# Preparing the down projection's weight sums one gate/up pair earlier in a fused block kernel

## The chip, the cores and the metric

The kernel runs on one core of a Trainium2 chip. The metric is the device time of one execution in microseconds (us), as a median of several runs; beside it stands one profiled execution, whose trace is what is read here.

## The reference

One layer of a streaming encoder on a sequence of 1024 rows with D = 1024, all in float32:

```
h  = rms_norm(x, norm1_w) * (1 + scale1) + shift1
x  = x + gate1 * hybrid_mixer(h, ...)          # gated delta rule + short conv, then w_out
h  = rms_norm(x, norm2_w) * (1 + scale2) + shift2
x  = x + gate2 * swiglu(h, w_gate, w_up, w_down)
return rms_norm(x, norm_f_w)

def swiglu(h, w_gate, w_up, w_down):
    return (jax.nn.silu(h @ w_gate) * (h @ w_up)) @ w_down
```

`shift`, `scale` and `gate` come from the vector c. w_gate and w_up are 1024 x 2816, w_down is 2816 x 1024. Everything that follows is in `swiglu`.

## The kernel before

**Products.** Every float32 operand is split into a high part (a cast to a rounded float32 that TensorE multiplies fast) and a low remainder; a product is three matmuls (high-high, high-low, low-high). A cast of the high part is ScalarE's (ACT), the subtraction that gives the low part VectorE's (DVE). The large matrix products are done by a seven-product scheme on 2 x 2 blocks (Strassen's in Winograd's form): sums of blocks (`S1` to `S4` of the left operand, `T1` to `T4` of the right) take the place of the eighth product.

**Gate and up.** The 2816 hidden columns are cut into `NP = 11` pairs of 128-column tiles. The loop `for p in range(1, NP)` goes through pairs 1 to 10, each in seven steps `s = 0..6`. A step loads (`turn_load`, `Weights.load`), sends the DMAs that were put on the list `pend` (`flush`), issues its matmuls (`run`, `inner`, `inner2`) and then `block(p, s)`, which is the work of the other engines after that step: closing the accumulators, SiLU, the gate-times-up product, and the casts and remainders for pair p + 1. The products of pair p go to the DRAM scratch `am_scr`, as left operands of the down projection.

**Down.** After pair 10 the down phase runs through three chunks of pairs (4, 4 and 3). Its right operands are blocks of w_down: a row pair j has the quarters B11, B12, B21, B22 (`quarter(j, i)`, i = 0..3, each 128 x 512), and

```
T1 = B12 - B11     T2 = T1 - B22     T3 = B12 - B22     T4 = B21 + T2
```

These lie in the DRAM scratch `bm[j, name]`. For row pairs 0 to 7 (`j < NRAW`) the weights stay as they are, since gate2 is applied to the output of the first two chunks; for row pairs 8 to 10 the weights are multiplied by gate2 (`row(i)`) first. Row pairs 0 to 8 are prepared in pieces within the gate/up loop, in pair p = j + 2; row pairs 9 and 10 within the down phase (`prep_load`, `prep_gate`, `prep_sums`).

**A piece** is `load_one_part(j, i)`, which loads quarter i into a buffer, and `part_of(i)`, which for i = 0 and 3 makes the negative (`neg`) and puts stores on `pend`. Additions are done by accumulating DMAs from GpSimd's queue (POOL): an entry of `pend` with three members is sent there, all others go through SyncE's queue (SP). `part_sums(j, n)` puts the sums on the list that need no tile (for raw row pairs B12 and B21 go from w_down to `bm` straight).

**Buffers.** The pieces use a ring of three tiles (`ring3`, `raw0` to `raw2`), in turn with other users: `turn_load(p - 3)` loads a tile of x, and `turn1(p - 3)` at the end of step 2 transposes it (a DVE instruction) into the next ring tile, from where four small DMAs write it out. A new user of a ring tile waits until the earlier one's reads and DMAs are done. In a regular pair the ring goes: part 0, x tile, transposed tile, part 3.

**Order.** Each engine works in the order in which the program issues to it; SP issues the DMAs in order too and waits at each one for what it needs. The weights of pair p + 1 are loaded by SP at steps 3 and 5 of pair p (`R<-in_w_gate`, `R<-in_w_up`).

Of the kernel before, what the change touches and what calls it, by code (L numbers as in the profile page):

```python
# [13 lines left out]
ALU = mybir.AluOpType  # L14
# [37 lines left out]
def kernel(  # L52
# [1567 lines left out]
    for n, m in enumerate((4, 5, 6, 7, 0, 1, 2, 3)):  # L1620
# [5 lines left out]
        if n in (0, 4, 7):  # L1626
            i = {0: 1, 4: 2, 7: 3}[n]
# [327 lines left out]
    def row(i):  # L1955
        return gates[5][:, i % 2 * HT:(i % 2 + 1) * HT]
# [4 lines left out]

    def part_of(i):
        j, t = bd[i]
        if j < NRAW:
            neg = t
        else:
            DVE.tensor_tensor(t, t, row(i), ALU.mult)
            neg = ring3() if i in (0, 3) else None
        if i in (0, 3):
            ACT.mul(neg, t, -1.0)  # L1970
        if i == 0:
            pend.append((bm[j, "T1"], neg))
        elif i == 1:
            pend.append((bm[j, "T3"], t))
            pend.append((bm[j, "T1"], t, 1))
        elif i == 3:
            pend.append((bm[j, "T2"], neg))
            pend.append((bm[j, "T3"], neg, 1) if j >= NRAW else (bm[j, "T3"], neg))
        else:
            pend.append((bm[j, "T4"], t))  # L1980
        if j >= NRAW and i != 1:
            pend.append((bm[j, {0: "B11", 2: "B21", 3: "B22"}[i]], t))

    def part_sums(j, n):
        b12, b21 = quarter(j, 1), quarter(j, 2)
        if n == 0 and j < NRAW:
            pend.extend([(bm[j, "T4"], b21), (bm[j, "T1"], b12, 1)])
        elif n == 1:
            if j < NRAW:
                pend.append((bm[j, "T3"], b12, 1))  # L1990
            pend.append((bm[j, "T2"], bm[j, "T1"], 1))
        elif n == 2:
            pend.append((bm[j, "T4"], bm[j, "T2"], 1))

    def prep_load(j, get):
        for fi in (0, 1):
# [20 lines left out]
    def block(p, s):  # L2017
        w, n = W.get(p), W.get(p + 1)
        last = p == NP - 1
        if s == 0:  # L2020
            if p > 0:
                o = p - 1
                a12 = c[o]["z5"][1]
                ACT.activation(a12, bk[o][0]["X"], AF.Silu)
                if w and p > 1:
                    w.cast("S2", 0)
                    w.cast("S2", 1)
                DVE.tensor_tensor(a12, bk[o][1]["X"], a12, ALU.mult)
                store(o, "A12", a12)
            if p == 1:  # L2030
                w.sum_n("S1")
                w.sum_n("S2")
                w.mat("S2")
            elif w:
                w.inner_low(2)
                w.inner_low(3)
                w.low("S2", 0)
                w.low("S2", 1)
                act(p - 1, "u2")
        elif s == 1:  # L2040
            if p < 2:
                keep(p, "p1", "X")
                rest0()
                w.cast("S1", 0)
                w.cast("S1", 1)
            elif w:
                w.sum_n("S4")
                w.sum_n("S1")
                w.mat("S1")
                sums_u2(p - 1)  # L2050
            if p > 0:
                o = p - 1
                a11, s1, a21 = c[o]["p1"][0], c[o]["p1"][1], c[o]["u2"][0]
                DVE.tensor_tensor(a11, a11, s1, ALU.subtract)
                DVE.tensor_tensor(a21, c[o]["z5"][1], a11, ALU.add)
                store(o, "S2", a11)
                store(o, "S4", a21)
            if p == 1:
                w.low("S1", 0)
                w.low("S1", 1)  # L2060
                w.sum_n("S3")
            if 1 < p < NP:
                part_of(0)
                part_sums(p - 2, 0)
            if p == 2:
                inner_t(1)
        elif s == 2:
            if p < 2:
                close(p, "p1", "Y")
            else:  # L2070
                close_inner(p, "p1")
            w.cast("S3", 0)
            silu(p, "p1")
            w.cast("S3", 1)
            w.low("S3", 0)
            w.low("S3", 1)
            act(p, "p1")
            store(p, "A11", c[p]["p1"][0])
            if p == 1:
                w.sum_n("S4")  # L2080
            if 3 <= p:
                turn1(p - 3)
        elif s == 3:
            keep(p, "u2", "X")
            if p >= FIRST2:
                w.inner_sums("S4")
                for i in range(4):
                    w.inner_cast(i)
                    w.inner_low(i)
                w.iu2 = w.iu  # L2090
            else:
                w.mat("S4")
            if p == 2:
                inner_t(2)
            if p == 3:
                inner_t(4)
        elif s == 4:
            keep(p, "z5", "Z")
            w.mat("A22")
            if p > 1:  # L2100
                if last:
                    part_of(1)
                else:
                    part_of(3)
                    part_sums(p - 2, 1)
            if n:
                n.mat("A11")
                if p != FIRST2:
                    n.sum_n("S3")
            if last:  # L2110
                first_mats(0, "A11", am_scr)
        elif s == 5:
            if p:
                close(p, "z5", "X")
            silu(p, "z5")
            act(p, "z5")
            if p == FIRST2:
                n.sum_n("S3")
            store(p, "A22", c[p]["z5"][0])
            if last:  # L2120
                part_of(3)
                part_sums(p - 2, 1)
                part_of(2)
            if p > 1:
                part_sums(p - 2, 2)
            if p == 2:
                inner_t(3)
            if last:
                first_mats(1, "B11", None)
        elif s == 6:  # L2130
            if p >= FIRST2:
                close_inner2(p)
            else:
                close(p, "u2", "Z")
            if n and p:
                n.inner_sums()
                n.inner_cast(0)
            elif n:
                n.cast("A12", 0)
            if p < FIRST2:  # L2140
                silu(p, "u2")
            if n and p:
                n.inner_cast(1)
                n.inner_low(0)
                n.inner_low(1)
            elif n:
                n.cast("A12", 1)
                n_slot[0] += 2
                n.low("A12", 0)
                n.low("A12", 1)  # L2150
            if n and p:
                n.inner_cast(2)
                n.inner_cast(3)
                n.sum_n("S2")
            if last:
                act(p, "u2")
                sums_u2(p)
            if last:
                first_mats(2, "A12", am_scr)
# [195 lines left out]

    for p in range(1, NP):
        for s in range(7):
            if p > 1 and s in (0, 3):
                load_one_part(p - 2, 1 if p == NP - 1 and s else s)
            if p == NP - 1 and s == 4:  # L2360
                load_one_part(p - 2, 3)
                load_one_part(p - 2, 2)
            if 3 <= p and s == 1:
                turn_load(p - 3)
            if s == 3 and p < NP - 1:
                W[p + 1] = Weights(p + 1)
                W[p + 1].load(0)
            if s == 5 and p < NP - 1:
                W[p + 1].load(1)
            if p == NP - 1 and s in (3, 5, 6):  # L2370
                first_load(*{3: (0, "A11"), 5: (1, "B11"), 6: (2, "A12")}[s])
            if s != 6 or p > 1:
                flush()
            if s == 1 and p > 1:
                keep(p, "p1", "X")
                inner(p, ("m1", "m2", "m5", "m6", "m3"))
            elif s == 2 and p > 1:
                run(p, s, (0,))
                inner(p, ("m7",))
                run(p, s, (1,))  # L2380
                inner(p, ("m4",))
            elif s == 5 and p >= FIRST2:
                inner2(p, ("m1", "m5", "m2", "m6", "m3", "m4"))
            elif s == 6 and p >= FIRST2:
                run(p, s, (0,), (0, 1))
                inner2(p, ("m7",))
                run(p, s, (0,), (2, 3))
                run(p, s, (1,))
            else:
                run(p, s)  # L2390
            block(p, s)
            if p == 1 and s in LATE:
                LATE[s]()
# [219 lines left out]
```

## Time and profile before

| | |
|---|---|
| median of 3 runs | 1151.91 us (1151.44 to 1152.65) |
| profiled execution | 1151.3 us, span 1149.5 us |
| busy: PE, its weight loads, DVE, ACT, POOL | 1136.6, 961.0, 962.4, 606.2, 92.3 us |
| pairs 1 to 10 of gate/up | about 556 to 930.5 us of the span |
| down phase | about 930.5 us to the end |

PE is TensorE, PEld its weight loads, SPq SyncE's queue. A row of the timeline gives a start, a duration, the engine, the operation, `out<-in` by the program's names (buffer numbers left out), and in brackets the idle time before it with what ended that. Steps of a pair last 5.4 us of PE, some with smaller matmuls a little more or less; pair 9 begins at 855.8 us and pair 10 at 893.2 us.

### The profile page before, as it was taken

To read this page: it belongs to the slowest core of one execution; us is meant where nothing else is said; L and a number is where in the kernel's file an instruction comes from. 1 tells how busy PE (TensorE), PEld (TensorE's weight loads), DVE (VectorE), ACT (ScalarE), POOL (GpSimd) and SP (SyncE) were. 2 spreads that over 40 slices of the span, in tenths; PEclk is the share of its full clock that TensorE was granted. 3 is DMA by queue.
4 is the path that set the end of the run, shared out by engine and by line. 5 is a ranking of instruction groups with operands and counts; after the bars stand their busy time and mean duration, and the time that the engine had idled before them with its cause. 6 is when DMAs were issued, how large, how long until landed. Compare 5 with 4: busy or idle time off the path is not lost.

```text
span 1149.5 us, 17231 instructions
## 1 busy us (share of the span) xinstructions
PE 1136.6 (99%) x5744; PEld 961.0 (84%) x5744; DVE 962.4 (84%) x1933; ACT 606.2 (53%) x1330; POOL 92.3 (8%) x129
## 2 busy tenths in 40 slices
PE   9999999999999999999999999999999999999997
PEld 7888888888888888888888888888888888888885
DVE  7898779799899787599989998878887977689976
ACT  7688743457743544255444545545455557454343
POOL 0001000100100101000000010101010000000302
PEclk9999999999999999999999999999999999999999
DMA  9931364743446582450336676866677599869933
GB/s 368 351 108 58 100 212 130 210 137 101 144 134 202 169 290 65 71 156 4 136 110 204 165 192 173 230 190 184 174 204 218 155 295 382 268 174 353 295 130 147
DMA packets 162634, 212.36 MB, mean 185 GB/s; under 512 B 54512, under 2 KB 79088, under 8 KB 162544
## 3 DMA queue, kind: packets, MB, share of 16 engines
q1 hardware_dynamic: 152656, 197.03, 52.7%
q0 software_dynamic: 7488, 13.63, 7.5%
q8 instruction: 45, 0.74, 0.3%
q10 hardware_dynamic: 2400, 0.59, 0.2%
q14 instruction: 45, 0.37, 0.1%
HBM read 161.40 MB, written 60.82 MB: 193 GB/s over the span
## 4 chain that ended last, share of the span: by engine, by line
PE 91%; DMA 4%; DVE 3%; ACT 1%; issue 1%; SPq 0%; POOL 0%; ACTq 0%; DVEq 0%; POOLq 0%
PE acc L87 34%; PE acc L449 24%; PE dn L87 18%; PE o L87 4%; PE o L449 3%; PE A L449 1%; PE K L449 1%; DMA raw<-in_w_in_dram 1%; DMA xbd<-dx 1%; PE w L449 1%; PE u L449 1%; PE qk L449 1%; PE kk L449 1%; DMA raw<-in_w_out_dram 1%; PE O L449 1%
## 5 line engine op out<-in xcount | busy, mean ns | idle before, releaser
L449 PE MATMUL acc<-h,u 128*128 128x512 f32 x1200 | 292.3, 396 | 0.0
L449 PEld LDWEIGHTS acc<-h,u 128*128 128x128 f32 x1200 | 220.9, 188 | 43.3 <-issue 0.5
L87 PE MATMUL acc<-h,hl 128*128 128x512 f32 (+1 forms) x540 | 109.0, 353 | 0.0
L87 PEld LDWEIGHTS acc<-h,hl 128*128 128x128 f32 x540 | 90.2, 189 | 15.0 <-issue 0.5
L87 PE MATMUL acc<-h,u 128*128 128x512 f32 (+1 forms) x516 | 100.3, 345 | 0.0
L87 PE MATMUL acc<-T,hl 128*128 128x512 f32 x408 | 97.5, 390 | 0.3 <-DVE T L88 0.3
L87 PEld LDWEIGHTS acc<-h,u 128*128 128x128 f32 x516 | 84.6, 189 | 12.6
L87 PE MATMUL dn<-h,h 128*128 128x512 f32 x396 | 91.5, 390 | 0.8 <-ACT h L88 0.6
L87 PE MATMUL acc<-T,u 128*128 128x512 f32 x384 | 91.1, 390 | 0.0
L87 PEld LDWEIGHTS dn<-h,h 128*128 128x128 f32 x396 | 74.2, 188 | 17.3 <-ACT h L88 1.0
L87 PEld LDWEIGHTS acc<-T,hl 128*128 128x128 f32 x408 | 75.3, 188 | 15.7 <-DVE T L88 0.8
L87 PEld LDWEIGHTS acc<-T,u 128*128 128x128 f32 x384 | 71.1, 188 | 13.9
L449 ACT CAST u<-raw 128x512 fp32r<-128x512 f32 x66 | 40.6, 620 | 57.1 <-PE acc L449 56.8
L449 DVE TENSOR_TENSOR u<-raw,u 128x512 fp32r<-128x512 f32 x82 | 55.9, 684 | 10.4 <-ACT u L449 10.2
L88 DVE TENSOR_TENSOR xo<-xo,dn 128x512 f32<-128x512 f32 x68 | 46.2, 682 | 14.8 <-PE dn L87 14.3
L88 ACT COPY L<-acc 128x256 f32<-128x256 f32 x68 | 25.3, 373 | 63.1 <-PE acc L87 62.8
L88 ACT CAST h<-rw 128x512 fp32r<-128x512 f32 x60 | 35.1, 620 | 40.8 <-PE dn L87 27.6
L449 DVE SCALAR_TENSOR_TENSOR cv<-pr,cols_a,cv 128x512 f32<-128x512 f32 x72 | 52.8, 746 | 1.7 <-ACT cv L449 1.5
L449 DVE SCALAR_TENSOR_TENSOR raw<-raw,cb 128x512 f32<-128x512 f32 x64 | 43.7, 682 | 10.9 <-DMA raw<-in_w_mod_dram 10.9
L88 DVE TENSOR_TENSOR h<-rw,h 128x512 fp32r<-128x512 f32 x60 | 39.5, 686 | 12.4 <-ACT h L88 12.4
L88 DVE TENSOR_TENSOR cc<-cc,acc 128x512 f32<-128x512 f32 x66 | 41.3, 644 | 6.7 <-PE acc L87 6.7
L88 ACT COPY cc<-acc 128x512 f32<-128x512 f32 x64 | 35.1, 583 | 19.8 <-PE acc L87 19.8
(391 smaller groups left out, 2222.3 us busy)
## 6 DMA issues: line engine op xcount, KB each, us to landing
raw<-in_w_in_dram SPq DMA_DIRECT2D x82, 256.0 KB, 3.0
am_scr<-cc SPq DMA_DIRECT2D x75, 256.0 KB, 2.1
raw<-in_w_mod_dram SPq DMA_DIRECT2D x64, 256.0 KB, 3.2
rw<-am_scr SPq DMA_DIRECT2D x53, 256.0 KB, 5.3
R<-in_w_gate_dram SPq DMA_DIRECT2D x22, 512.0 KB, 5.3
R<-in_w_up_dram SPq DMA_DIRECT2D x22, 512.0 KB, 5.7
rw<-bm SPq DMA_DIRECT2D x43, 256.0 KB, 5.3
wa<-in_w_mod_dram SPq DMA_DIRECT2D x16, 512.0 KB, 9.8
```

Of the source, the lines that this page charges most:

```text
L87: return call(*a, **k)
L88: ins = call(*a, **k)
L449: ins = call(*a, **k)
```

## The change

Row pairs 0 to 7 are prepared in pair p = j + 1 instead of j + 2, so row pair 0 in pair 1, where nothing was prepared before. Row pair 8, the gated one, was prepared as a whole in pair 10; now parts 0 and 1 come in pair 9, and parts 3 and 2 in pair 10. For it the negative is no longer ACT's, made from the gated tile, but DVE's, made from the raw tile in one instruction (times -1, times gate) into its own ring tile, ahead of the multiplication in place. For raw row pairs ACT's negation in place stays.

```diff
     def part_of(i):
         j, t = bd[i]
+        neg = t
         if j < NRAW:
-            neg = t
+            ACT.mul(t, t, -1.0)
         else:
+            if i in (0, 3):
+                neg = ring3()
+                DVE.scalar_tensor_tensor(neg, t, -1.0, row(i), ALU.mult, ALU.mult)
             DVE.tensor_tensor(t, t, row(i), ALU.mult)
-            neg = ring3() if i in (0, 3) else None
-        if i in (0, 3):
-            ACT.mul(neg, t, -1.0)
...
+    def part_step(p, n):
+        j = min(p - 1, NRAW)
+        if p == 1:
+            if n == 1:
+                part_of(0)
+                part_sums(j, 0)
+            elif n == 2:
+                part_of(3)
+                part_sums(j, 1)
+                part_sums(j, 2)
+        elif p <= NRAW:
+            if n < 2:
+                part_of(3 * n)
+            part_sums(j, n)
+        elif n < 2:
+            part_of(n if p == NRAW + 1 else 3 - n)
+            if p > NRAW + 1:
+                part_sums(j, 1 + n)
+
+    def part_load(p, s):
+        j = min(p - 1, NRAW)
+        if p == 1:
+            for i in (0, 3) if s == 3 else ():
+                load_one_part(j, i)
+        elif s in (0, 3):
+            load_one_part(j, s if p <= NRAW else {0: 0, 3: 1}[s] if p == NRAW + 1 else {0: 3, 3: 2}[s])
```

In `block`, `part_step(p, 0)` stands in step 1, `part_step(p, 1)` in step 4 and `part_step(p, 2)` in step 5, in the places of the old calls; the last pair's extra `part_of` calls in steps 4 and 5 are gone. In the loop `part_load(p, s)` takes the place of the old loads at steps 0, 3 and (last pair) 4.

ACT at the end of pair 10, before. `cc<-cc` is a SiLU, `raw_9295<-raw_9191` the negation of part 3 of row pair 8, the `h_1` casts are the first B11 of the down phase (loaded into `R`), the `L` copies belong to pair 10's inner products:

```order
L88 COPY L_9250<-acc_9248 128x256
L88 ACTIVATE cc_9219<-cc_9219 128x512
L88 ACTIVATE raw_9295<-raw_9191 128x512
L88 CAST h_1_1497_9298<-R_9241 128x512
L88 CAST h_1_1498_9299<-R_9241 128x512
L88 CAST h_1_1499_9300<-R_9241 128x512
L88 CAST h_1_1500_9301<-R_9241 128x512
```

The same place now:

```order
L88 COPY L_9261<-acc_9259 128x256
L88 ACTIVATE cc_9229<-cc_9229 128x512
L88 CAST h_1_1497_9305<-R_9251 128x512
L88 CAST h_1_1498_9306<-R_9251 128x512
L88 CAST h_1_1499_9307<-R_9251 128x512
L88 CAST h_1_1500_9308<-R_9251 128x512
L88 COPY L_9261<-acc_9259 128x256
```

The negation between the SiLU and the casts is gone.

DVE in step 1 and 2 of pair 9, before: products of pair 8 being summed, then the closing of an accumulator of pair 9 (`cc` with `L` and `acc`), the remainders of S3 (`hl`), and the transpose:

```order
L88 TENSOR_TENSOR cc_8448<-cc_8492,cc_8301 128x512
L88 TENSOR_TENSOR cc_8661<-cc_8661,L_8672 128x512
L88 TENSOR_TENSOR cc_8661<-cc_8661,L_8672 128x256
L88 TENSOR_TENSOR cc_8661<-cc_8661,acc_8665 128x512
L88 TENSOR_TENSOR cc_8661<-cc_8661,L_8672 128x256
L88 TENSOR_TENSOR cc_8661<-cc_8661,acc_8664 128x256
L88 TENSOR_TENSOR hl_8762<-R_8414,hl_8762 128x512
L88 TENSOR_TENSOR hl_8765<-R_8414,hl_8765 128x512
L88 TENSOR_TENSOR cc_8661<-cc_8661 128x512
L88 STREAM_TRANSPOSE raw_8770<-raw_8658 128x512
```

The same place now, with the gated part 0 of row pair 8 (`raw_8633`) and its negative (`raw_8726`):

```order
L88 TENSOR_TENSOR cc_8462<-cc_8506,cc_8315 128x512
L88 SCALAR_TENSOR_TENSOR raw_8726<-raw_8633,gate_4513 128x512
L88 TENSOR_TENSOR raw_8633<-raw_8633,gate_4513 128x512
L88 TENSOR_TENSOR cc_8675<-cc_8675,L_8686 128x512
L88 TENSOR_TENSOR cc_8675<-cc_8675,L_8686 128x256
L88 TENSOR_TENSOR cc_8675<-cc_8675,acc_8679 128x512
L88 TENSOR_TENSOR cc_8675<-cc_8675,L_8686 128x256
L88 TENSOR_TENSOR cc_8675<-cc_8675,acc_8678 128x256
L88 TENSOR_TENSOR hl_8777<-R_8428,hl_8777 128x512
L88 TENSOR_TENSOR hl_8780<-R_8428,hl_8780 128x512
L88 TENSOR_TENSOR cc_8675<-cc_8675 128x512
L88 STREAM_TRANSPOSE raw_8785<-raw_8672 128x512
```

Two instructions came in ahead of the closing; `raw_8785`, into which the transpose writes, is the ring tile that `raw_8633` had.

SP at the same time (steps 2 and 3 of pair 9), before: T1 of row pair 7 (`bm_124`) and its T4 (a copy from DRAM to DRAM), the load of part 3, then pair 10's weights:

```order
L88 DMA am_scr<-cc_8448 128x512
L88 DMA bm_124<-raw_8619 128x512
L88 DMA bm_127<-in_w_down_dram 128x512
L88 DMA raw_8772<-in_w_down_dram 128x512
L88 DMA R_8774<-in_w_gate_dram 128x4x256
L88 DMA R_8774<-in_w_up_dram 128x4x256
```

Now: T1 and B11 of row pair 8 (`bm_131`, `bm_135`), the load of part 1, then pair 10's weights:

```order
L88 DMA am_scr<-cc_8462 128x512
L88 DMA bm_131<-raw_8726 128x512
L88 DMA bm_135<-raw_8633 128x512
L88 DMA raw_8787<-in_w_down_dram 128x512
L88 DMA R_8789<-in_w_gate_dram 128x4x256
L88 DMA R_8789<-in_w_up_dram 128x4x256
```

The number of DMAs is the same here; the load now goes into the ring tile that the x tile had, which the transpose reads.

More of the change, by code (lines that the diff above doesn't have):

```diff
@@ L2062, in block @@
             if 1 < p < NP:
-                part_of(0)
-                part_sums(p - 2, 0)
+                part_step(p, 0)
             if p == 2:
@@ L2099, in block @@
             w.mat("A22")
[L2100 to L2105, printed above, removed]
+            part_step(p, 1)
             if n:
@@ L2119, in block @@
             store(p, "A22", c[p]["z5"][0])
[L2120 to L2125, printed above, removed]
+            part_step(p, 2)
             if p == 2:
@@ L2357 @@
         for s in range(7):
[L2358 to L2362, printed above, removed]
+            part_load(p, s)
             if 3 <= p and s == 1:
```

## The prediction

> **What bounds the kernel now.** I read the page's busy line and clock first, then the waits of TensorE (PE) from pair 1 to the end, then its busy time in three stretches, and last the instructions around the one place where it stood still.
>
> ```profile
> PE 1136.6 (99%) x5744; PEld 961.0 (84%) x5744; DVE 962.4 (84%) x1933; ACT 606.2 (53%) x1330; POOL 92.3 (8%) x129
> PEclk9999999999999999999999999999999999999999
> ```
>
> PE is busy 99% of a span of 1149.5 us, at full granted clock in every slice. Since a busy PE can hide a short wait, I look at what it waited for in the stretch that the change touches (from 545 us on) and behind it:
>
> ```profile
> PE dn L87 <- ACT h L88: 0.6, 1, 0.6
> PE acc L87 <- DVE T L88: 0.3, 1, 0.3
> PE dn L87 <- DVE h L88: 0.2, 1, 0.2
> ```
> ```profile
> 551.25:930.50 379.25, 379.25 (x2006) 327.91 (x2006) 319.55 (x544) 186.33 (x370) 27.61 (x33) 1.00 0.66 180
> 930.50:932.10 1.60, 0.77 (x3) 0.27 (x2) 0.83 (x2) 1.60 (x4) 0.89 (x1) 1.00 1.04 398
> 932.10:1141.90 209.80, 209.80 (x923) 172.91 (x923) 170.86 (x274) 103.25 (x200) 24.65 (x38) 1.00 0.80 256
> ```
>
> The first number behind the comma is PE's busy time: 379.25 of 379.25 us through pairs 1 to 10, 0.77 of 1.60 at the hand-over to the down phase, 209.80 of 209.80 to its last matmul. So all that an edit of pairs 1 to 10 can give back is 1.60 - 0.77 = 0.83 us, and all it can otherwise do is cost. The 0.3 us on T lie in pair 0, ahead of everything moved.
>
> The hand-over, in the instructions of PE, ScalarE (ACT), SyncE's queue (SP) and VectorE (DVE):
>
> ```profile
> 926.44 4.24 PE L87 MATMUL acc<-T,hl 128*128 128x512 f32 x18
> 931.29 0.50 PE L87 MATMUL dn<-h,h 128*128 128x512 f32 x1 [0.61 <-ACT h L88]
> 932.02 1.19 PE L87 MATMUL dn<-h,h 128*128 128x512 f32 x4 [0.22 <-DVE h L88]
> ```
> ```profile
> 923.37 0.64 ACT L88 ACTIVATE cc<-cc 128x512 f32<-128x512 f32 x1
> 930.10 0.63 ACT L88 ACTIVATE raw<-raw 128x512 f32<-128x512 f32 x1 [6.09 <-DMA bm<-raw]
> 930.64 1.64 ACT L88 CAST h<-R 128x512 fp32r<-128x512 f32 x3
> ```
> ```profile
> 917.77 4.04 SPq L88 DMA_DIRECT2D raw<-in_w_down_dram  x2
> 921.91 1.80 SPq L88 DMA_DIRECT2D R<-in_w_down_dram  x4
> ```
> ```profile
> 924.65 0.68 DVE L88 TENSOR_TENSOR raw<-raw,gate 128x512 f32<-128x512 f32 x1
> 926.14 0.69 DVE L88 TENSOR_TENSOR raw<-raw,gate 128x512 f32<-128x512 f32 x1 [0.81 <-issue]
> 931.27 1.29 DVE L88 TENSOR_TENSOR h<-R,h 128x512 fp32r<-128x512 f32 x2 [4.44 <-DMA R<-am_scr]
> ```
>
> ACT's negation of part 3 of row pair 8 waits 6.09 us for a ring buffer (its earlier content must land in `bm` first). Behind it in ACT's queue stand the casts of the down phase's first B11, and PE's first `dn` matmul starts only when the first cast is done: it starts at 930.64 and ends near 931.25, while PE is free at 926.44 + 4.24 = 930.68. VectorE's remainders (`h<-R,h`, 931.27) follow the casts.
>
> **The change, part by part.**
>
> 1. *Pair 10's end.* Removed: two loads (SP 917.77, 4.04 us, the second waiting for its buffer), two gate multiplies (DVE 924.65 and 926.14), and the negation (ACT 930.10) with its 6.09 us wait. The order now has ACT's casts of B11 right behind the SiLU of 923.37, that is from 924.0, if the data are there: their loads move up by those 4.04 us, from 921.91 to about 917.9. Rows that touch R put a landing between 2.9 and 8.4 us, with a median of 5.6:
>
> ```profile
> DMA to landing us min/median/max: 2.9/5.6/8.4
> ```
>
> With the median the first of the four lands at 923.5, the last (issued 1.4 us later) at about 925; four casts of 0.55 us are done by 927, the remainders by 928. PE needs them at 930.5. With the longest landing the first is there at 926.3 and its cast at 927. Both ends leave the wait at nothing: **-0.83 us**. Next late would be A12 and B21 for the second product, 48 matmuls (11 us) later; their loads stand behind the same removed work on SP and move up with it.
>
> 2. *Pair 9 now does part 0 gated.* Added to VectorE ahead of pair 9's closing adds: one scalar_tensor_tensor (the negated product) and one multiply; ACT loses a negation there and one four stages on, where VectorE gets a multiply (part 1). Prices:
>
> ```profile
> L88 DVE SCALAR_TENSOR_TENSOR xo<-xo,fst,nfb 128x512 f32<-128x512 f32 x14 | 10.0, 748 | 0.0
> L88 ACT ACTIVATE raw<-raw 128x512 f32<-128x512 f32 x18 | 11.5, 637 | 10.2 <-DMA bm<-raw 6.1 <-DVE raw L88 4.1
> ```
>
> 0.75 for the first (same operands, two tensors and a scalar) and 0.68 for the multiply: 1.43 us on VectorE at 869.15, where these follow:
>
> ```profile
> 869.15 1.02 DVE L88 TENSOR_TENSOR cc<-cc,L 128x512 f32<-128x512 f32 x2
> 871.98 0.42 DVE L88 TENSOR_TENSOR cc<-cc,acc 128x256 f32<-128x256 f32 x1 [0.88 <-PE acc L87]
> 872.32 1.29 DVE L88 TENSOR_TENSOR hl<-R,hl 128x512 fp32r<-128x512 f32 x2
> 874.13 0.71 DVE L88 STREAM_TRANSPOSE raw<-raw 128x512 f32<-128x512 f32 x1
> ```
> ```profile
> 877.25 5.60 PE L87 MATMUL acc<-T,hl 128*128 128x512 f32 x24
> ```
>
> 0.88 us of idle time before 871.98 takes the most of it, so 0.55 us goes on. The S3 remainders (`hl<-R,hl`) end at 874.1 instead of 873.6, and PE reads them at 877.25: 3 us of cover, cost 0. In pair 10 the scalar_tensor_tensor adds 0.75 us at the same place, with the same cover. The multiply of part 1 falls where VectorE waited for ACT's casts of `hl<-R` (the 880.21 row below).
>
> 3. *The transpose and SP's queue in pair 9.* The extra ring tile makes the transpose reuse part 0's buffer, so VectorE waits there until part 0 is stored as B11; and the load of part 1 goes into the buffer that the transpose reads, so SP now waits for the transpose, with pair 10's first gate and up weights behind it. Where pair 10 does the same today, the two stores landed in
>
> ```profile
> DMA to landing us min/median/max: 2.0/2.2/2.3
> ```
>
> Over all of `bm`, it is 2.0 to 7.4:
>
> ```profile
> DMA to landing us min/median/max: 2.0/5.2/7.4
> ```
>
> The nearest row is pair 10's, with the same pair of stores. Issued at 869.15 + 1.43 = 870.6, B11's lands at 872.9 and the transpose doesn't wait: 874.7 to 875.4. The load goes at 875.4, gate weights at 875.85 and up at 876.3, 2.2 us later than here:
>
> ```profile
> 873.64 0.38 SPq L88 DMA_DIRECT2D R<-in_w_gate_dram  x1
> 874.07 0.50 SPq L88 DMA_DIRECT2D R<-in_w_up_dram  x1
> DMA to landing us min/median/max: 5.9/6.4/6.9
> ```
> ```profile
> 880.21 0.62 ACT L88 CAST hl<-R 128x512 fp32r<-128x512 f32 x1 [0.39 <-PE acc L87]
> 882.93 0.62 ACT L88 CAST hl<-R 128x512 fp32r<-128x512 f32 x1 [2.10 <-PE acc L87]
> 883.60 0.37 ACT L88 COPY L<-acc 128x256 f32<-128x256 f32 x1
> ```
> ```profile
> 884.84 0.88 PE L87 MATMUL acc<-t,hl 128*128 128x256 f32 x6
> ```
>
> With 5.9 and 6.9 the gate half lands at 881.8, the up half at 883.2. The second cast waits 0.3 us longer, and ACT's copy behind it ends at 884.2, where PE accumulates on at 884.84: 0.6 us to spare, cost 0. In the worst case (7.4 for the store, 8.4 for the weights) the transpose starts at 878.0, up goes at 879.65 and lands at 888.05, the copy ends at 889.05: **+4.2 us**. A copy from DRAM to DRAM and an accumulating DMA that ran beside these weights are gone in pair 9, so I stay with 0.
>
> 4. *Pair 1 gets the first row pair's preparation.* Two loads on SP ahead of pair 2's gate weights, two negations of 0.64 us on ACT; four plain DMAs (SP) and four accumulating ones (POOL) follow. The buffers are free (the stores before the loads on SP already wait for their last reader), so the loads go in the gap in which SP waits for the weights' buffer:
>
> ```profile
> 567.44 3.86 SPq L88 DMA_DIRECT2D am_scr<-cc  x5
> 575.82 0.38 SPq L88 DMA_DIRECT2D R<-in_w_gate_dram  x1
> ```
>
> That is 4.5 us for two issues. ACT has room:
>
> ```profile
> 581.79 0.62 ACT L88 CAST hl<-R 128x512 fp32r<-128x512 f32 x1 [0.50 <-DMA R<-in_w_up_dram]
> 586.61 0.63 ACT L88 ACTIVATE cc<-cc 128x512 f32<-128x512 f32 x1 [4.20 <-DVE cc L88]
> ```
>
> One negation falls ahead of a cast that waits for its DMA anyway, the other behind a wait of 4.20. If that cover were gone, it would be 2 x 0.64 = 1.3 us at most. Cost 0. Pairs 2 to 8 do the same as before for the next row pair, with ring buffers turned by one. Row pair 8's four accumulating DMAs on POOL, before all in pair 10, stand one in pair 9 and three in pair 10; nobody but the down phase's third chunk reads them.
>
> Sum: -0.83 + 0 + 0 + 0. Profiled time 1151.3 (span 1149.5 and 1.8 around it) becomes 1150.5; the median of the runs lies 0.6 above the profiled time, so **1151.1 us**.
>
> [...] By the busy line VectorE has 84% and ACT 53%, and the change gives VectorE two negations of 0.75 us that ACT did. [...]
>
> **The rivals.**
>
> - *The hand-over stall stays in another form* (the first `dn` matmul waits for B11's DMA, or its bank): no change, 1151.9. For it: the DMA engines are at 1.04 in that stretch, and the row of 931.27 names a DMA. Against: the casts follow ACT's 930.10 without a gap.
> - *Slower, through pair 9's queue*: the transpose waits for the store, SP for the transpose, pair 10's weights come late. It starts to cost when the up half lands after about 883.8, 0.6 us beyond my estimate, and reaches +4.2 - 0.83: 1152 to 1155.3. For it: landings up to 7.4 and 8.4 exist in this trace. Against: the same stores took 2.3 in pair 10, and less DMA traffic.
> - *VectorE decides*: its two negations show in full, 1151.9 - 0.8 + 1.5 = 1152.6. For it: 84% busy. Against: PE never waited for it in 379 us.
>
> **How the numbers follow.** Forecast 0.66, stall stays 0.15, pair 9's queue 0.13, VectorE 0.06. A measurement tells about 0.2% from no change, 2.3 us here. The forecast's 0.8 us is far inside; a gain over 0.2% has no room on PE, so 0.04 is only for runs that come out apart. Slower by over 0.2% needs 3.1 us of new stall: half of the queue's 0.13 and a little for an unseen wait, 0.08. The rest, 0.88, is the same. Low end: the forecast less the 1.2 us between the slowest and fastest run shown, 1149.9. High end: the rivals up to most of the queue's span, 1154.2.
>
> **What would show it.** Right: no PE wait for `h` at the first `dn` matmul, no negation on ACT after pair 9 begins, ACT's casts of B11 starting near 924 to 926; SP's gate weights in pair 9 at about 875.9 and PE without a gap at 884.84. Wrong: a PE wait in pair 9 or 10 released by ACT's `L` copy, a gap on VectorE before pair 9's transpose, or a PE wait in pair 1.

## The result and the profile after

| | before | after |
|---|---|---|
| median | 1151.53 us (1149.89 to 1154.08, 22 runs) | 1149.45 us (1148.08 to 1151.81, 22 runs) |
| profiled span | 1149.5 us | 1146.7 us |

The ratio is 0.998, with a 95% interval from 0.9973 to 0.9986; a second comparison of the same two kernels gave 0.9981 (0.9972 to 0.9989). All ratios compare fast runs, so one run of the experiment e5 (1916.36 us, at a granted clock of 0.557) counts in none. The change makes the kernel faster by 2.1 us by the medians. The forecast was 0.8 us, and the median lies 0.45 us below the low end of the range. What the change was said to do it does; how much that is worth was read too small.

The page's busy line after, and all that TensorE (PE) waited for from 545 us on:

```profile
PE 1135.6 (99%) x5744; PEld 960.9 (84%) x5744; DVE 964.3 (84%) x1935; ACT 605.8 (53%) x1328; POOL 92.3 (8%) x129
```
```profile
PE acc L87 <- DVE T L88: 0.3, 1, 0.3
```

Both waits for `h` at the hand-over are gone, and no new one has come. The same by stretches: pairs 1 to 10, and the down phase.

```profile
550.33:929.50 379.17, 379.17 (x2006) 328.11 (x2007) 324.50 (x552) 188.03 (x373) 30.13 (x36) 1.00 0.67 186
929.50:1139.20 209.70, 209.70 (x925) 173.18 (x924) 168.36 (x270) 102.98 (x197) 22.64 (x36) 1.00 0.77 249
```

PE's timeline at the hand-over, after:

```profile
925.47 4.24 PE L87 MATMUL acc<-T,hl 128*128 128x512 f32 x18
929.55 21.92 PE L87 MATMUL dn<-h,h 128*128 128x512 f32 x96
951.31 9.00 PE L87 MATMUL dn<-wu,hl 128*128 128x512 f32 x39
```

and before, the first row of the products that follow, which the prediction did not look at:

```profile
954.01 6.28 PE L87 MATMUL dn<-wu,hl 128*128 128x512 f32 x27
```

I call the time from the start of the 18 matmuls to the first `dn<-wu,hl` the hand-over. After it is 951.31 - 925.47 = 25.84 us: 114 matmuls at 0.2267 (0.39 us each in the rows; `RS<-raw,ones`, a 128x512 matmul of unrounded float32, takes 0.59). Before it was 954.01 - 926.44 = 27.57. **The hand-over was worth 1.73 us, not 0.83.** The rows of PE's weight loads (PEld) show where the rest lay. Before:

```profile
931.29 0.19 PEld L87 LDWEIGHTS dn<-h,h 128*128 128x128 f32 x1 [1.03 <-ACT h L88]
932.02 10.76 PEld L87 LDWEIGHTS dn<-h,h 128*128 128x128 f32 x48 [0.54 <-DVE h L88]
943.19 10.56 PEld L87 LDWEIGHTS dn<-h,h 128*128 128x128 f32 x47 [0.41 <-DVE h L88]
```

By starts, PE lost 0.77 before the first `dn` matmul (931.29 instead of 926.44 + 4.08), 0.50 before the second (932.02 instead of 931.29 + 0.23), and 0.46 from there to 954.01: the 95 matmuls take 21.99 and not 95 x 0.2267 = 21.53. By the single starts in the trace 0.15 of that is a wait at 943.19, near the start of the second product, which reads B21 (its remainder was late). The rest lies right behind the two waits of 932.02 and 943.19, where matmuls first start 0.33 and then 0.23 apart. The matmul rows showed 0.61, 0.22 and nothing, since a matmul's modelled end (0.39 to 0.50 us behind its start) covers up to two more starts. After, the weight loads run through:

```profile
929.33 21.72 PEld L87 LDWEIGHTS dn<-h,h 128*128 128x128 f32 x96
```

ScalarE (ACT) and SyncE's queue (SP) at the place, after:

```profile
922.40 0.64 ACT L88 ACTIVATE cc<-cc 128x512 f32<-128x512 f32 x1
922.93 1.14 ACT L88 CAST h<-R 128x512 fp32r<-128x512 f32 x2
924.88 0.62 ACT L88 CAST h<-R 128x512 fp32r<-128x512 f32 x1 [0.81 <-DMA R<-in_w_down_dram]
927.31 0.62 ACT L88 CAST h<-R 128x512 fp32r<-128x512 f32 x1 [1.81 <-DMA R<-in_w_down_dram]
```
```profile
918.32 3.19 SPq L88 DMA_DIRECT2D R<-in_w_down_dram  x4
928.68 1.76 SPq L88 DMA_DIRECT2D R<-in_w_down_dram  x4
```

B11's casts follow the SiLU and wait only for their data, the last until 927.31, 1.6 us ahead of PE. B21's loads (the second row) go at 928.68.

### The profile page after: what moved, and what is told of

It is laid out like the page before. It is cut to its first block, busy times and chain, and to the rows that moved or that the text cites. A ratio compares the mean times of both kernels' runs of the same rounds, so it can differ in the third digit from the quotient of the medians.

```text
span 1146.7 us, 17231 instructions
## 1 busy us (share of the span) xinstructions
PE 1135.6 (99%) x5744; PEld 960.9 (84%) x5744; DVE 964.3 (84%) x1935; ACT 605.8 (53%) x1328; POOL 92.3 (8%) x129
## 4 chain that ended last, share of the span: by engine, by line
PE 92%; DVE 3%; DMA 3%; ACT 1%; issue 1%; SPq 0%; DVEq 0%; ACTq 0%
PE acc L87 35%; PE acc L449 24%; PE dn L87 18%; PE o L87 4%; PE o L449 4%; PE K L449 1%; DMA raw<-in_w_mod_dram 1%; PE A L449 1%; PE ab L449 1%; PE qk L449 1%; PE kk L449 1%; PE O L449 1%; DMA raw<-in_w_out_dram 1%; DVE xo L88 1%; DMA raw<-y_scr 0%
```

## A ledger for the experiments

Profiled spans of one kernel differ by some us (1146.7 and 1150.7 for the changed one). Nearly all of that lies ahead of pair 1, in code that no kernel here but one changes. So I take as a mark PE's start behind the wait for T in pair 0 (551.25 before, 550.33 after) and compare what follows. "Pair 9" is the loss by starts there: the time from the 18 `acc<-T,u` that end pair 8 to the 18 in pair 9, less the 37.34 us that it takes before (851.76 to 889.10) and after (850.79 to 888.13). Spans are read to 0.1 us.

| kernel | hand-over | pair 9 | mark to end | to before | ratio of times, interval |
|---|---|---|---|---|---|
| before | 27.57 | 0 | 598.25 | | |
| after | 25.84 | 0 | 596.37 | -1.88 | 0.998 (0.9973 to 0.9986) |
| after, again | 25.84 | 0 | 596.41 | -1.84 | 0.9981 (0.9972 to 0.9989) |
| e1, own tile | 25.84 | 0 | 596.50 | -1.75 | 0.9985 (0.9976 to 0.9993) |
| e2, casts first | 27.40 | 0 | 598.01 | -0.24 | 1.0006 (0.9998 to 1.0015) |
| e3, VectorE negates | 29.54 | 0 | 599.99 | +1.74 | 1.0012 (1.0003 to 1.002) |
| e4, ACT negates | 25.84 | 0 | 596.57 | -1.68 | 0.9985 (0.9976 to 0.9993) |
| e5, row pairs 0 to 7 | 26.76 | 0 | 597.22 | -1.03 | 0.9995 (0.9987 to 1.0004) |
| e7, late weights | 25.84 | 2.22 | 598.53 | +0.28 | 0.9999 (0.9989 to 1.0009) |
| e8, VectorE +2.04 | 25.84 | 1.13 | 597.65 | -0.60 | 0.9991 (0.9982 to 1.0) |
| e9, VectorE +4.1 | 25.84 | 3.54 | 599.91 | +1.66 | 1.0012 (1.0002 to 1.0022) |

Less the hand-over and pair 9, mark to end is 570.45 to 570.73 in all eleven. Behind the mark these two columns are all that differs, to 0.3 us. (e6 edits the code at the mark and stands by itself.)

## The experiments

**e1: take away only the wait.**

```diff
-            neg = ring3() if i in (0, 3) else None
+            neg = xq.tile([P, 2, HT], F32, name=nm("ng"), tag="cc", bufs=4)[:, 0] if i == 3 else ring3() if i == 0 else None
```

> The kernel before, but the negative of part 3 in pair 10 goes to a tile of its own and no longer waits for a ring buffer; nothing else is changed, all loads and the other preparation stay where they were. I measure the hand-over from the start of the 18 matmuls acc<-T,hl that end pair 10 to the first matmul dn<-wu,hl: 27.57 us before, 25.84 after the change (114 matmuls at 0.2267). Theory (the whole gain is the hand-over, lost to the 6.09 us for which ACT's negation stood ahead of B11's casts): the casts start by 928 instead of 930.64, the hand-over takes 25.8 to 26.3, the time falls by 1.3 to 1.7 us, ratio 0.9985 to 0.9989. Rival A (the gain is in what moved out of pair 10 or in pairs 1 to 9): hand-over within 0.3 of 27.57, ratio 1.000. Rival B (B11's loads, 4 us later here than after the change, then hold the casts): hand-over 26.8 to 27.5, ratio 0.9993 to 1.0.

```profile
924.92 0.63 ACT L88 ACTIVATE ng<-raw 128x512 f32<-128x512 f32 x1 [1.36 <-DVE raw L88]
925.84 1.24 ACT L88 CAST h<-R 128x512 fp32r<-128x512 f32 x2 [0.28 <-DMA R<-in_w_down_dram]
```

The tile comes from another ring, of four buffers (`cc`). In the timeline of ACT the negation comes at 924.92 instead of 930.10, and the trace names VectorE as what it waited for; the casts follow. Hand-over 25.84, ratio 0.9985: the theory's numbers. That one wait carries the whole hand-over loss; neither the loads' place nor pairs 1 to 9 are needed for it.

**e3: VectorE negates, nothing is moved.**

```diff
+            if i in (0, 3):
+                neg = ring3()
+                DVE.scalar_tensor_tensor(neg, t, -1.0, row(i), ALU.mult, ALU.mult)
             DVE.tensor_tensor(t, t, row(i), ALU.mult)
-            neg = ring3() if i in (0, 3) else None
-        if i in (0, 3):
+        if i in (0, 3) and j < NRAW:
             ACT.mul(neg, t, -1.0)
```

> The kernel before with only the other half of the change: row pair 8 stays whole in pair 10, but its two negatives come from VectorE's scalar_tensor_tensor ahead of the gate multiply, none from ACT. Theory (it is the wait for the ring buffer that costs, whoever waits): the wait of 4 to 6 us moves to VectorE, where two gate multiplies (0.68 each) and B11's remainders stand behind it, so the first dn matmul starts without a wait, but the second group waits for the remainders until about 933: hand-over 27.5 to 29, ratio 1.0 to 1.0012. Rival (VectorE in place of ACT is what helps): hand-over 25.8 to 26.3, ratio 0.9985.

VectorE's wait, then PE's (timeline), then PE's busy time in two stretches, with the granted clock in the third column from the end:

```profile
930.14 0.69 DVE L88 SCALAR_TENSOR_TENSOR raw<-raw,gate 128x512 f32<-128x512 f32 x1 [5.31 <-DMA bm<-raw]
```
```profile
930.63 0.39 PE L87 MATMUL dn<-h,h 128*128 128x512 f32 x1
932.82 23.44 PE L87 MATMUL dn<-h,h 128*128 128x512 f32 x95 [1.80 <-DVE h L88]
956.09 4.24 PE L87 MATMUL dn<-wu,hl 128*128 128x512 f32 x18
```
```profile
930.66:934.07 3.41, 1.61 (x7) 1.00 1.03 376
934.07:937.48 3.41, 3.41 (x9) 0.50 1.06 300
```

The ring buffer's wait now stands in VectorE's queue, ahead of B11's remainders, as the theory had it; the negation's engine alone gains nothing. But the hand-over is 29.54, over the expected 29. The wait is 1.96 us by starts, and another 1.74 are lost where PE shows no idle time: the 95 matmuls take 956.09 - 932.82 = 23.27 us and not 95 x 0.2267 = 21.53. The granted clock says why: 1.25 us behind the pause it falls to 0.50, for 3.41 us, half of which is 1.71.

**e4: the move without VectorE's negation.** In the changed kernel the negative is ACT's again, from the gated tile:

```diff
-            if i in (0, 3):
-                neg = ring3()
-                DVE.scalar_tensor_tensor(neg, t, -1.0, row(i), ALU.mult, ALU.mult)
             DVE.tensor_tensor(t, t, row(i), ALU.mult)
+            if i in (0, 3):
+                neg = ring3()
+                ACT.mul(neg, t, -1.0)
```

> The changed kernel, but the negatives of row pair 8 are ACT's again, from the gated tile, as before; only the move to pair 9 and 10 is left of the change. Theory (the move takes the negation out of the way of B11's casts; who negates does not matter): hand-over 25.84, ratio as the change's, 0.9973 to 0.9986. Rival (the negation on VectorE brings the gain): hand-over over 27, ratio 0.9995 to 1.0. If ACT's queue is in the way in pair 9 (the negation ahead of the L copies or of the casts of S3), PE shows a wait in pair 9 of up to 1 us and the ratio is 0.999.

Hand-over 25.84 and no other wait. With 0.9985 against 0.998 and 0.9981 the intervals overlap: which engine negates isn't seen in the time.

**e5: only row pairs 0 to 7 move.** Pair 9 prepares nothing, pair 10 all of row pair 8 as before; the same shift is made in steps 4 and 5.

```diff
-            if 1 < p < NP:
+            if 1 < p <= NRAW or last:
                 part_of(0)
-                part_sums(p - 2, 0)
+                part_sums(p - 1 if p <= NRAW else NRAW, 0)
...
-            if p > 1 and s in (0, 3):
-                load_one_part(p - 2, 1 if p == NP - 1 and s else s)
+            if p == 1 and s == 3:
+                load_one_part(0, 0)
+                load_one_part(0, 3)
+            elif 1 < p <= NRAW and s in (0, 3):
+                load_one_part(p - 1, s)
+            elif p == NP - 1 and s in (0, 3):
+                load_one_part(p - 2, 1 if s else 0)
```

> Only the move of row pairs 0 to 7 by one pair (pair 1 prepares row pair 0, pair 8 row pair 7, pair 9 nothing); row pair 8 is prepared whole in pair 10 by the old instructions. Theory: no gain from pairs 1 to 9, the stall at the hand-over stays; hand-over 26.8 to 28.5 (its ring tiles are turned differently), ratio 0.9995 to 1.0005. Rival (part of the gain comes from the regular pairs, for instance the 0.35 us by which the medians differ more than the hand-over does, or the 0.92 us by which the profiled run of the changed kernel enters pair 1 earlier): ratio 0.9985 to 0.9995 with the hand-over near 27.6.

```profile
929.39 0.63 ACT L88 ACTIVATE raw<-raw 128x512 f32<-128x512 f32 x1 [5.27 <-DMA bm<-raw]
```

The negation still waits, 5.27 us instead of 6.09, so that the hand-over loses 0.92 instead of 1.73. Nothing came from pairs 1 to 9, as expected; the ratio can't be told from 1. The hand-over lies 0.04 under the span that I had written.

**e2: the other order.** Before, with `first_mats(1, "B11", None)` ahead of part 3's `part_of(3)`:

```diff
             if last:
+                first_mats(1, "B11", None)
                 part_of(3)
...
-            if last:
-                first_mats(1, "B11", None)
```

> The kernel before with one edit of order: in pair 10 the casts and remainders of B11 are issued ahead of part 3's gate multiply and negation; the wait for the ring buffer and all loads stay. Theory (only what stands behind the waiting negation in ACT's queue matters): casts start when the loads land, near 927, first dn matmul without a wait, hand-over 25.84 to 26.4, ratio 0.9985 to 0.999. Rival (the wait itself, or the late part 3, costs at whatever place it stands): it moves to A12's casts behind it, with a PE wait near 943, hand-over 26.6 to 27.6, ratio 0.9992 to 1.0.

```profile
931.04 12.40 PE L87 MATMUL dn<-h,h 128*128 128x512 f32 x54
944.17 0.49 PE L87 MATMUL dn<-h,h 128*128 128x512 f32 x1 [0.73 <-ACT h L88]
```
```profile
931.97 1.79 SPq L88 DMA_DIRECT2D bm<-raw  x4
933.81 3.28 SPq L88 DMA_DIRECT2D R<-in_w_down_dram  x4
```
```profile
943.50 1.14 ACT L88 CAST h<-R 128x512 fp32r<-128x512 f32 x2 [2.94 <-DMA R<-in_w_down_dram]
```

The kernel before, SP and VectorE:

```profile
933.80 2.43 SPq L88 DMA_DIRECT2D R<-in_w_down_dram  x4
931.27 2.50 DVE L88 TENSOR_TENSOR h<-R,h 128x512 fp32r<-128x512 f32 x4 [4.44 <-DMA R<-am_scr]
```

Here my theory fell and its rival held, though it named A12's casts and not B21's. The first product starts without a wait, but the second stops at 944.17 for B21's casts, which wait for DMA: on SP, B21's loads (933.81) stand behind part 3's stores, which need the late negative (931.97). Hand-over 27.40. In e2 the negation is late because its gate multiply now stands behind B11's remainders on VectorE, so e2 does not test the ring buffer's wait alone; and B21's slowest load landed in 8.7 us, against 7.0 before, so a part of the 27.40 may be that execution's. That the gain is gone is also what the 11 runs say (1.0006). In the kernel before the loads went at 933.80 as well, behind part 3's stores (930.76 to 932.58) and then behind B11's remainders (done at 933.77, after the late casts); the wait at 943.19 was what the first stall had left to be seen. So the late negation holds up two queues, ACT's and, through its store and the late casts, SP's. e1 and the change free both (B21's loads at 930.82 and 928.68).

**e7: the pair-9 rival made true.** In the changed kernel pair 10's first weights are loaded one step later:

```diff
-            if s == 3 and p < NP - 1:
+            if s == (4 if p == 9 else 3) and p < NP - 1:
```

> The changed kernel with pair 10's first weights loaded one step later in pair 9, behind the four stores of the transposed tile on SyncE's queue, so about 4.5 us later (up weights issued near 879.6 instead of 875.13): this is the state that the prediction's worst case for pair 9's queue described. Theory (that rival is a real mechanism with a cover that the change did not use up): the up half lands near 886, ACT's L copy ends near 887, and PE, at 883.87 in the changed kernel, waits 2.5 to 4 us in pair 9; hand-over 25.84; 0.8 to 2.3 us slower than before, ratio 1.0007 to 1.002. Rival (these loads are hidden anyway): no PE wait, ratio 0.9985.

```profile
879.23 0.43 SPq L88 DMA_DIRECT2D R<-in_w_gate_dram  x1
879.70 0.52 SPq L88 DMA_DIRECT2D R<-in_w_up_dram  x1
```
```profile
885.07 0.62 ACT L88 CAST hl<-R 128x512 fp32r<-128x512 f32 x1 [0.87 <-DMA R<-in_w_up_dram]
```
```profile
886.01 0.98 PE L87 MATMUL acc<-t,hl 128*128 128x256 f32 x6 [1.95 <-ACT L L88]
```

The mechanism is real: cast, `L` copy, PE. Its price is lower than expected: 2.22 us by starts for 4.57 us of delay on SP, and +0.28 to before where 0.8 to 2.3 were written. The up half was cast 5.4 us after its issue, and in the changed kernel 7.2 (875.13 to 882.31).

**e8 and e9: VectorE's cover in pair 9.** The negated product of part 0 is written four and seven times instead of once:

```diff
-                DVE.scalar_tensor_tensor(neg, t, -1.0, row(i), ALU.mult, ALU.mult)
+                for _ in range(7 if i == 0 else 1):
+                    DVE.scalar_tensor_tensor(neg, t, -1.0, row(i), ALU.mult, ALU.mult)
```

> The changed kernel with VectorE's negated product of part 0 in pair 9 written four times instead of once (the same values): 3 x 0.68 = 2.04 us more VectorE work at 868.9. It measures the cover that the prediction claimed there. Theory: the S3 remainders (873.0 in the changed kernel) have 3.2 us until PE reads them at 876.28, so no wait there; but the transpose and SyncE's queue behind it, with pair 10's weights, move 2 us, and of their cover 0.7 us is left (second cast's L copy ends 883.19, PE needs it by 883.9): a PE wait for L of 0.7 to 1.4 us near 884, none elsewhere; ratio 0.9986 to 0.9994. Rival (VectorE at 84% has no room and the work shows in full): 2.0 us, ratio 0.9998 to 1.0.

```profile
884.63 0.98 PE L87 MATMUL acc<-t,hl 128*128 128x256 f32 x6 [0.82 <-ACT L L88]
```

> The same with seven times instead of once: 6 x 0.68 = 4.1 us more. Theory: the cover of 3.2 us at the S3 remainders is used up, PE waits 0.7 to 1.1 us at 876.3 for hl, and then for L near 884 another 1.5 to 2.8 us: 2.4 to 3.6 us in all, ratio 1.0002 to 1.0016. Rival (the work shows in full): 4.1 us, ratio 1.0016 to 1.0022.

```profile
877.15 5.76 PE L87 MATMUL acc<-T,hl 128*128 128x512 f32 x24 [0.76 <-ACT cc L88]
887.24 0.98 PE L87 MATMUL acc<-t,hl 128*128 128x256 f32 x6 [2.18 <-ACT L L88]
```

2.04 us more cost 1.13, 4.1 more cost 3.54 (by starts 0.98 at the wait in e8, 0.94 + 2.34 at the two in e9, the rest right behind them): within what the theory had. Near half of the small dose is hidden, and in e8 PE waits through SP's queue and the weights, not for VectorE's own results. In e9 at 877.15 the trace names ACT's `cc` copies, not the `hl` remainders that I had written: they stand behind a SiLU that VectorE delayed.

**The change again, and a try at more.**

> The changed kernel once more, unaltered, to settle whether its first comparison (0.998) holds more than the hand-over gives. Theory (all of the gain is the hand-over, 27.57 to 25.84): 1.73 us, ratio 0.9985, profiled hand-over 25.84. Rival (a second gain of some 0.35 us or more elsewhere): ratio 0.998 or below again.

0.9981 once more, hand-over 25.84. The 1.73 us (0.9985) lie within both intervals, but both middles are lower, while e1 and e4, which lose nothing at the hand-over either, gave 0.9985; see the last section.

In e6, pair 0's second half of A22 is cast one step later:

```diff
-            if n == 3 and k == 0:
-                for q in (0, 1):
-                    W[0].cast("A22", q)
-                    w_low("A22", q)
+            if n == 3 and k in (0, 1):
+                W[0].cast("A22", k)
+                w_low("A22", k)
```

> A try at a better version: the changed kernel, and in pair 0 the cast and remainder of the second half of A22 are issued one step later, so that the second T4 tile is ready 0.6 us sooner; PE waits there for T at 550.33 (4 matmuls after 548.86 would end their issue at 549.77, so 0.56 us by starts). Expected: that wait falls to 0 to 0.1, 0.3 to 0.56 us less than the changed kernel, hand-over 25.84, ratio 0.9980 to 0.9983. Rival: the wait moves to the second half's first matmul (its remainder is now the late one), 0.2 to 0.5 us, ratio 0.9985.

```profile
550.70 6.17 PE L87 MATMUL acc<-T,hl 128*128 128x512 f32 x24
556.70 3.61 PE L87 MATMUL acc<-h,hl 128*128 128x512 f32 x15
```

PE's list of waits is empty now, yet the 24 matmuls take 6.00 us from start to start instead of 24 x 0.2267 = 5.44; in the changed kernel it is 6.14 (548.86 to 555.00). The wait broke into small ones that only the weight loads show. 0.14 us, ratio 0.9985 (0.9977 to 0.9994): no gain. The changed kernel stays the best version.

## Why the prediction was right and wrong

1. *Pair 10's end* (-0.83): right in mechanism, wrong in size. The step that failed is "all that an edit of pairs 1 to 10 can give back is 1.60 - 0.77 = 0.83 us": it took the busy time of an engine whose rows overlap (0.39 to 0.50 us each, 0.2267 from start to start) for its work. By starts it is 0.77 + 0.50 = 1.27 at the hand-over itself. And "A12 and B21 for the second product ... move up with it" took them for work in time; B21 was already late, and between the second `dn` matmul and 954.01 another 0.46 were lost, 0.15 of it waiting for B21 and the rest in restarts. Together 1.73. The casts began at 922.93, in an execution that runs 0.97 us ahead of the one before, so at 923.9 by the forecast's times (924 to 926). The low end of the range rested on that false bound, with only the spread of the runs below it; so did the sentence that a larger gain "has no room on PE". But the bound isn't all of the miss: with 1.73 the forecast would have been 1150.2, inside the range. The measured 1149.45 lies 0.75 lower. Of that, 0.38 is chance in the starting point, since the median before was 1151.91 in three runs and is 1151.53 in 22; the other 0.35 stays open. The resolution of 0.2% was too coarse as well: the interval is 0.0013 wide.
2. *Pair 9 on VectorE* (0): right. After:

```profile
868.17 0.68 DVE L88 SCALAR_TENSOR_TENSOR raw<-raw,gate 128x512 f32<-128x512 f32 x1
868.89 0.69 DVE L88 TENSOR_TENSOR raw<-raw,gate 128x512 f32<-128x512 f32 x1
871.37 0.41 DVE L88 TENSOR_TENSOR cc<-cc,acc 128x256 f32<-128x256 f32 x1
871.70 1.32 DVE L88 TENSOR_TENSOR hl<-R,hl 128x512 fp32r<-128x512 f32 x2
873.53 0.71 DVE L88 STREAM_TRANSPOSE raw<-raw 128x512 f32<-128x512 f32 x1
```

   The scalar_tensor_tensor took 0.68, not 0.75; the 0.88 us of idle time ahead of the last add is used up, and the remainders end at 873.0, 3.3 us before PE's 876.28. VectorE's 84% is a share of the whole span; where the work went it had those 0.88 us, and of 2.04 us more 0.91 stayed hidden (e8).
3. *Pair 9's queue* (0): right, and narrow as said. The transpose has no wait in the row above; SP's rows:

```profile
874.27 0.33 SPq L88 DMA_DIRECT2D raw<-in_w_down_dram  x1
874.70 0.39 SPq L88 DMA_DIRECT2D R<-in_w_gate_dram  x1
875.13 2.24 SPq L88 DMA_DIRECT2D R<-in_w_up_dram  x1
```
```profile
882.31 0.62 ACT L88 CAST hl<-R 128x512 fp32r<-128x512 f32 x1 [1.53 <-DMA R<-in_w_up_dram]
882.83 0.36 ACT L88 COPY L<-acc 128x256 f32<-128x256 f32 x1
```
```profile
883.87 0.88 PE L87 MATMUL acc<-t,hl 128*128 128x256 f32 x6
```

   PE is 0.97 us earlier here than before, so gate and up go 2.0 us later against it (2.2 forecast), and 0.7 us are left between the copy and PE (0.6 forecast). The worst case of +4.2 was too high: with the up weights issued as late as it assumed (879.70 against 879.65), e7 lost 2.22.
4. *Pair 1* (0): right; e5 does this move alone, with no wait there.

## What to carry over

Read a stall on an engine whose rows overlap, as PE's do here, by starts: count the instructions between two places, multiply by the pitch that the same form has in an undisturbed stretch, and compare; idle time between modelled ends showed 0.83 of 1.73 us here, and none of 0.56 in e6. When an instruction waits, follow every queue that its result feeds as well as the one it stands in: changing only the order behind it (e2) moved the stall, taking away what it waited for (e1) removed it. A cover can be measured by putting known work into it (e8, e9), and what runs out first need not be the engine that got the work.

## What was not expected of the hardware

- Matmul rows and weight-load rows give two different losses for one stall: 0.83 and 1.03 + 0.54 + 0.41 = 1.98, with 1.73 by starts between them. For this stall the matmul rows show 0.90 too little, and the weight loads 0.25 too much.
- A pause of 1.96 us by starts went ahead of a lower clock in e3 (0.50 for 3.41 us, at a price of 1.74 us); pauses of 2.11 and 2.34 us in e7 and e9 did not: the clock stayed at 1.00 (to 910 and 895 us). By these traces the length of a pause alone does not tell which it will be. In the second run of the changed kernel the clock fell as well, at 390.19, behind a pause of 1.81 us; in e3 the pause at the same place was 1.76 us, and the clock stayed at 1.00 (to 400 us). Of the 3.41 us ahead of the fall PE's rows show 1.61 us busy in e3 and 1.60 in the second run of the changed kernel; of 3.41 us at the second pause of e9 they show 1.69, and no fall followed. The second run of the changed kernel, then e9:

```profile
386.78:390.19 3.41, 1.60 (x13) 1.00 0.62 211
390.19:393.60 3.41, 3.41 (x16) 0.50 0.28 82
```
```profile
885.51:888.92 3.41, 1.69 (x14) 1.00 1.08 189
888.92:892.34 3.42, 3.42 (x23) 1.00 0.96 293
```

  What else decides it, these rows do not show.
- Whether the 0.35 us by which the medians differ more than the hand-over does have to do with the clock is open. Of the runs of the kernel before whose clock is on record, 15 of 91 had a mean granted clock of 0.997 or less, and took 1153.8 us in the mean against 1151.3 for the others; of the kernels without a stall behind the mark (after, again, e1, e4, e6) it was 3 of 67. 12% fewer runs with 2.4 us more are 0.3 us in the mean. But a link is not shown, and the traces speak against it: the hand-over of the kernel before has 0.83 us of idle time in all, at a granted clock of 1.00 (926.44 to 954.01), and in the three profiled executions of these two kernels the only fall ahead of the end lies ahead of the mark (390.19). The 0.35 may also be noise: e1, e4 and e6, likewise without the stall, gave 0.9985, which is the hand-over alone.
